# The first 256 columns of gate and up by token, one unit of sums for two, and another order of the splits, in a two-layer macaron block in fp32

## The chip, the cores and the metric

The kernel runs on one core of a Trainium2 chip. The metric is the device time of one execution in microseconds, as the median of several runs. Five engines share the work, each with a program of its own in fixed order: TensorE (PE) multiplies, VectorE (DVE) and ScalarE (ACT) do elementwise work and empty PSUM, GpSimd (POOL) does next to nothing here, and SyncE (SP) issues the loads. Semaphores alone tie them together, so an instruction that waits holds up everything behind it on its own engine.

## The reference

x has 256 tokens of 1024 features, everything is fp32, and there are two layers. Each has a feed-forward, a mixer and a second feed-forward, all with a residual. What the change touches is the feed-forward, of which there are four:

```python
def rms_norm(x, g):
    y = xf * lax.rsqrt(jnp.mean(xf * xf, axis=-1, keepdims=True) + RMS_EPS)
    return (y * g.astype(jnp.float32)).astype(x.dtype)

def swiglu(x, w_gate, w_up, w_down):          # 1024 -> 2816 -> 1024
    return (jax.nn.silu(x @ w_gate) * (x @ w_up)) @ w_down

for layer in range(DEPTH):                    # DEPTH = 2
    x = x + 0.5 * swiglu(rms_norm(x, ffn_norm[layer, 0]), ...)
    h = rms_norm(x, mix_norm[layer])
    x = x + (hybrid_ab_mixer(h, ...) if layer % 2 == 0 else short_conv_mixer(h, ...))
    x = x + 0.5 * swiglu(rms_norm(x, ffn_norm[layer, 1]), ...)
return rms_norm(x, final_norm)
```

The hybrid mixer of layer 0 multiplies `gelu(u)` into chunks mixed over the tokens, and has an attention beside it; both are concatenated and projected.

## The kernel before

**Products in parts.** A product in fp32 is made of products of rounded parts. Every weight tile of 1 MB is loaded raw by SP, rounded to `whi` by ACT (`Weights.high`, L91), and what the rounding left is taken to `wlo` by DVE (`Weights.low`, L96). The activations have the same two parts. With x as the stationary operand (`mm_n`, L290) a product takes three matmuls of 512 columns: hi by hi, hi by lo, lo by hi. With the weights stationary (`mm_t`, L267) it takes one of 512 columns (both parts of x at once) and one of 256.

**The stream of weights.** All weight tiles stand in one list of `Item`s. `W.next()` hands out the next one, and first issues the high parts of three items ahead and the low parts of two (`catch_up`, L106). There are five raw buffers; the low part of an item frees its buffer, and the next load goes into it. So the order of the list is the order of splits on ACT and DVE and of loads on SP. An item can also ask for sums of raw tiles, made on DVE (L87).

**A feed-forward.** Its 2816 columns of gate and up are 256 columns of an opening and five units of 512. The opening has the tokens along the free dimension (`open_pairs`, L439): two PSUM pairs, added (`added`, L417), scaled by the norm's root broadcast to all partitions (`Norm.broadcast`, L375: a product with the diagonal of the roots), gated and split (`gated`, L516). The units have the tokens on the partitions, so the root is a column there (`Norm.column`, L365) and scales within the evacuation (`silu` L540, `times` L537); then four transposes per pair of 128 columns turn the result (`turn`, L524), which is split for the down projection. A plain unit (`plain`, L543) has four items, and each of its four steps makes 24 matmuls. A unit of sums (`summed`, L565) is a Strassen-like form: seven steps of 12 matmuls, from four loads, seven splits, four sums of weights and sums of x (`Sums`, L473). `ORDER` (L37) interleaves the steps of three plain units ("n") and two of sums ("s"), and with them the items. Transposes are put into a list, `later`, from which one entry is run behind each step and, at the end, one ahead of each half of a down projection.

**The start.** The first feed-forward opens while x and the first weights land. SP issues pieces of 256 KB alternately; PE transposes x piece by piece (`turn_x`, L757), ACT and DVE split it and the weights (`prepare`, L764), and the opening's products run over eight slices of the features.

**PSUM.** Three tiles `ps` of two banks go round, and two tiles `misc` of one.

Of the kernel before, what the change touches and what calls it, by code (L numbers as in the profile page):

```python
# [36 lines left out]
ORDER = "nnsnsnsnssnsnsnsnsnssnsssn"  # L37
# [10 lines left out]
class Weights:  # L48
# [13 lines left out]
    def load_piece(self, i, s, e):  # L62
        name, src = self.src[i]
        if name not in self.raw:
            tag = self.free.pop(0)
            self.raw[name] = self.pool.tile(list(src.shape), F32, tag=tag, bufs=1, name="raw"), tag
            self.loaded = i + 1
        self.nc.sync.dma_start(self.raw[name][0][:, s:e], src[:, s:e])

    def load(self):  # L70
        while self.loaded < len(self.src) and self.free:
            self.load_piece(self.loaded, 0, self.src[self.loaded][1].shape[1])
# [59 lines left out]
def block_kernel(ctx: ExitStack, tc: tile.TileContext, a, out):  # L132
# [26 lines left out]
    def chunk(src):  # L159
# [8 lines left out]
    def sum_unit(g, u, c):  # L168
# [3 lines left out]
        yield Item([(b11, u[:, lo, c])], b11, drop=[])  # L172
        yield Item([(b12, g[:, lo, c])], b11, [(b11, b11, b12, ALU.subtract)], drop=[])
        yield Item([(b22, g[:, hi, c])], b11, [(b11, b11, b22, ALU.subtract)], drop=[])
        yield Item([], b22, drop=[])
        yield Item([], b12, [(b12, b12, b22, ALU.add)], drop=[b12, b22])
        yield Item([(b21, u[:, hi, c])], b21, drop=[])
# [5 lines left out]
    def ffn_items(l, s, natural):  # L183
        g, u, d = (cols(a[n][l, s]) for n in ("ffn_w_gate", "ffn_w_up", "ffn_w_down"))
        yield chunk(g[:, :, :256])
        yield chunk(u[:, :, :256])
        plain = (i for j in (0, 2, 4) for i in plain_unit(g, u, unit_cols(j)))
        sums = (i for j in (1, 3) for i in sum_unit(g, u, unit_cols(j)))
        for c in ORDER:
            yield next(plain if c == "n" else sums)  # L190
# [191 lines left out]

    def residual(norm, y, scale):
# [64 lines left out]
    def t_pair(xs, mid=None, mm=None, p=None):  # L448
        w, p = W.next(), p or ps()
# [57 lines left out]
    def ffn(norm, nxt, hooks=None, opened=None, squares=None):  # L507
        h = [None] * FB
        later = []
# [6 lines left out]
        def gated(g, u):  # L516
            s, v = (by_token(x, norm.rbc, tag) for x, tag in ((g, "ev_g"), (u, "ev_u")))
            nc.scalar.activation(s, s, AF.Silu)
            nc.vector.tensor_tensor(v, s, v, op=ALU.mult)
            h[:2] = split(v, 0, True)  # L520

        def turned(v, f, n):

            def turn(q):  # L524
                m = misc(1)
                for b in range(2):
                    for t in range(NT):
                        o = (2 * q + b) * P
                        nc.tensor.transpose(m[:, b * S + t * P:b * S + (t + 1) * P], v[t][:, o:o + P], ident)
                h[f + 2 * q:f + 2 * q + 2] = split(m, f + 2 * q)  # L530

# [89 lines left out]
        def first():  # L621
            gated(g0, u0)
# [543 lines left out]
```

## Time and profile before

| | |
|---|---|
| median of the runs (lowest, highest) | 951.05 us (950.37, 951.75) |
| the profiled execution, and its span | 951.3 us, 949.6 us |
| PE busy | 923.6 us, 97% |
| DVE busy | 728.3 us, 77% |
| ACT busy | 505.1 us, 53% |
| share of the chain that ended last: PE, DVE, ACT | 65%, 23%, 6% |

PE matmuls overlap in their ends, so a PE that counts as busy may still be held to less than its peak: what counts is the distance from one start to the next. The share of DVE is a mean over stages: it is near full in the feed-forwards' units and half idle in the down projections. The four feed-forwards begin at 0, 293.6, 478.8 and 755.4 us.

### The profile page before, as it was taken

The page shows a single profiled execution, that of the slowest core. Times are in us where ns is not written, and L with a number is a line of the kernel's source. Part 1 is how long each engine was busy: PE and PEld are TensorE (multiplying, and loading weights), DVE is VectorE, ACT ScalarE, POOL GpSimd, SP SyncE. Part 2 cuts the span into 40 slices and gives each one's busy share as a digit, 9 for nine tenths or more (in the row PEclk, how much of TensorE's full clock was granted, in tenths as well). Part 3 has the DMA queues.
Part 4 walks back from the last instruction along what each step waited for, and adds up shares of the span by engine and source line. Part 5 has one row for each costly group of instructions (what it writes and reads, how often), then busy time and mean ns, then how long its engine had stood idle before and what let it go on. Part 6 is the DMA issues. An engine that isn't in the chain of part 4 may idle for free.

```text
span 949.6 us, 11856 instructions
## 1 busy us (share of the span) xinstructions
PE 923.6 (97%) x4916; PEld 788.6 (83%) x4916; DVE 728.3 (77%) x740; ACT 505.1 (53%) x510; POOL 2.0 (0%) x9
## 2 busy tenths in 40 slices
PE   8889999999999999999999999999999999999997
PEld 7668788888988777888888788888999888788786
DVE  6998996466768989885669899664587789999562
ACT  6656564354847646553455665443444465656342
POOL 0000000000000000000000000000000000000000
PEclk9999999999999999999999999999999999999999
DMA  9439286646354446585544465847445533838511
GB/s 326 162 99 324 89 287 195 226 156 233 104 175 133 132 172 227 170 284 167 200 151 137 155 241 167 278 159 242 155 162 185 196 111 124 297 124 283 182 67 45
DMA packets 121169, 173.82 MB, mean 183 GB/s; under 512 B 3408, under 2 KB 69532, under 8 KB 121116
## 3 DMA queue, kind: packets, MB, share of 16 engines
q1 hardware_dynamic: 120780, 172.53, 54.2%
q8 instruction: 38, 0.62, 0.3%
q10 hardware_dynamic: 336, 0.54, 0.2%
q14 instruction: 15, 0.12, 0.0%
HBM read 172.01 MB, written 1.05 MB: 182 GB/s over the span
## 4 chain that ended last, share of the span: by engine, by line
PE 65%; DVE 23%; ACT 6%; issue 4%; DMA 1%; SPq 0%; DVEq 0%; ACTq 0%
PE ps L278 12%; DVE wlo L96 10%; PE ps L293 9%; PE ps L294 9%; PE ps L292 8%; PE ps L280 6%; DVE raw L87 4%; PE ps L286 3%; PE ps L287 3%; PE ps L288 3%; PE ps L270 2%; PE misc L294 2%; PE misc L292 2%; PE misc L293 2%; ACT whi L91 2%
## 5 line engine op out<-in xcount | busy, mean ns | idle before, releaser
L96 DVE TENSOR_TENSOR wlo<-raw,whi 128x2048 fp32r<-128x2048 f32 (+2 forms) x196 | 422.9, 2175 | 23.3 <-ACT whi L91 23.1
L91 ACT ACTIVATE whi<-raw 128x2048 fp32r<-128x2048 f32 (+2 forms) x196 | 354.2, 1824 | 160.4 <-PE ps L278 44.7
L293 PE MATMUL ps<-wlo,x 128*128 128x512 f32 x512 | 200.7, 392 | 4.7 <-DVE wlo L96 4.7
L292 PE MATMUL ps<-whi,x 128*128 128x512 f32 x512 | 203.0, 396 | 0.0
L294 PE MATMUL ps<-whi,x 128*128 128x512 f32 x512 | 200.2, 391 | 0.0
L278 PE MATMUL ps<-hx,whi 128*128 128x512 f32 x528 | 166.8, 397 | 0.0
L280 PEld LDWEIGHTS ps<-hx,wlo 128*128 128x128 f32 x528 | 99.2, 188 | 23.4
L293 PEld LDWEIGHTS ps<-wlo,x 128*128 128x128 f32 x512 | 96.6, 189 | 26.3 <-DVE wlo L96 7.0
L294 PEld LDWEIGHTS ps<-whi,x 128*128 128x128 f32 x512 | 96.4, 188 | 20.4
L292 PEld LDWEIGHTS ps<-whi,x 128*128 128x128 f32 x512 | 96.6, 189 | 19.7
L280 PE MATMUL ps<-hx,wlo 128*128 128x256 f32 x528 | 103.8, 278 | 0.0
L386 DVE SCALAR_TENSOR_TENSOR xT<-ps,xT 128x512 f32<-128x512 f32 x40 | 27.4, 690 | 69.3 <-PE ps L280 61.3
L278 PEld LDWEIGHTS ps<-hx,whi 128*128 128x128 f32 x528 | 80.4, 189 | 0.0
L87 DVE TENSOR_TENSOR raw<-raw 128x2048 f32<-128x2048 f32 x32 | 73.2, 2288 | 2.7 <-DMA raw<-in_ffn_w_gate 2.2
L286 PE MATMUL ps<-x,whi 128*128 128x256 f32 x224 | 64.0, 286 | 0.0
L287 PE MATMUL ps<-x,whi 128*128 128x256 f32 x224 | 63.4, 283 | 0.0
L288 PE MATMUL ps<-x,wlo 128*128 128x256 f32 x224 | 63.4, 283 | 0.0
L404 DVE TENSOR_TENSOR hx<-misc,hx 128x512 fp32r<-128x512 f32 x40 | 27.5, 689 | 32.5 <-ACT hx L401 32.5
L270 PE MATMUL ps<-x,whi 128*128 128x512 f32 x128 | 45.4, 398 | 0.8 <-ACT whi L91 0.6
L287 PEld LDWEIGHTS ps<-x,whi 128*128 128x128 f32 x224 | 43.0, 192 | 0.0
L286 PEld LDWEIGHTS ps<-x,whi 128*128 128x128 f32 x224 | 42.9, 192 | 0.0
L288 PEld LDWEIGHTS ps<-x,wlo 128*128 128x128 f32 x224 | 42.9, 192 | 0.0
(244 smaller groups left out, 1130.1 us busy)
## 6 DMA issues: line engine op xcount, KB each, us to landing
raw<-in_ffn_w_gate SPq DMA_DIRECT2D x43, 1024.0 KB, 5.3
raw<-in_ffn_w_up SPq DMA_DIRECT2D x43, 1024.0 KB, 5.2
raw<-in_ffn_w_down SPq DMA_DIRECT2D x34, 1024.0 KB, 6.4
raw<-in_conv_w_in SPq DMA_DIRECT2D x12, 1024.0 KB, 5.3
raw<-in_hyb_w_in SPq DMA_DIRECT2D x10, 1024.0 KB, 6.7
raw<-in_ffn_w_down SPq DMA_DIRECT2D x12, 768.0 KB, 4.9
raw<-in_hyb_w_out SPq DMA_DIRECT2D x4, 1024.0 KB, 5.4
raw<-in_conv_w_out SPq DMA_DIRECT2D x4, 1024.0 KB, 5.8
```

The costliest lines, as they stand in the source:

```text
L87: self.nc.vector.tensor_tensor(self.raw[dst][0], self.raw[x][0], self.raw[y][0], op=op)
L91: self.nc.scalar.activation(self.part(i, "whi")[:, s:e], self.tile(i)[:, s:e], AF.Copy)
L96: self.nc.vector.tensor_tensor(lo[:, s:e], raw[:, s:e], hi[:, s:e].bitcast(F32), op=ALU.subtract)
L270: nc.tensor.matmul(dst, whi, x, start=start, stop=False, skip_group_check=True)
L278: nc.tensor.matmul(dst, ws[i][0], xs[i], start=start and i == 0, stop=False, skip_group_check=True)
L280: nc.tensor.matmul(dst[:, :S], ws[i][1], xs[i][:, :S], start=False, stop=stop and i == n - 1, skip_group_check=True)
L286: nc.tensor.matmul(dst[:, :S], whi, x[:, :S], start=start, stop=False, skip_group_check=True)
L287: nc.tensor.matmul(dst[:, :S], whi, x[:, S:], start=False, stop=False, skip_group_check=True)
L288: nc.tensor.matmul(dst[:, :S], wlo, x[:, :S], start=False, stop=stop, skip_group_check=True)
L292: nc.tensor.matmul(dst, xhi, whi, start=start, stop=False, skip_group_check=True)
L293: nc.tensor.matmul(dst, xhi, wlo, start=False, stop=False, skip_group_check=True)
L294: nc.tensor.matmul(dst, xlo, whi, start=False, stop=stop, skip_group_check=True)
```

## The change

Four things change.

1. The opening is made like the units, with the tokens on the partitions. An item of the opening is four slices of gate and up side by side (2 x 256 columns, two loads), and `opening` makes 3 matmuls of 512 columns per slice and token block. The result is scaled by the column of roots as it leaves PSUM (`first`: two `silu`, two `times` of 256 columns), and turned by four transposes. The broadcast goes from the four feed-forwards; in the later ones the column root now stands right behind the opening. The sums of x are made later in the first feed-forward.
2. The first feed-forward has four plain units and one of sums. Its order is `"nnnsnnsnnsnnsnnsnnsnnsn"`; the other three keep the old one.
3. At the down projection the left transposes come behind the first half, two sets at once, and alternate between the two `misc` tiles.
4. In the hybrid mixer the first gated half is made inside `mix`. The hooks of the first feed-forward (small loads, angles, tables) move to earlier steps.

```diff
-ORDER = "nnsnsnsnssnsnsnsnsnssnsssn"
+ORDERS = {"first": ((0, 1, 2, 4), (3,), "nnnsnnsnnsnnsnnsnnsnnsn"),
+          "other": ((0, 2, 4), (1, 3), "nnsnsnsnssnsnsnsnsnssnsssn")}
...
     def ffn_items(l, s, natural):
-        yield chunk(g[:, :, :256])
-        yield chunk(u[:, :, :256])
...
+        for k in range(0, KB, 4):
+            yield chunk(g[:, k:k + 4, :256], u[:, k:k + 4, :256])
...
+    def opening(norm, p, k, w):
+        for t in range(NT):
+            mm_n(p[:, t], x_at(norm, t, k), (w[0][:, k % 4], w[1][:, k % 4]), k == 0, k == KB - 1)
...
-            later.extend([None] * n + [lambda: turn(0)] + [None] * (2 - n) + [lambda: turn(1)])
+            fns = [lambda q=q: turn(v, f + 2 * q, q, misc(1 - q * free[0])) for q in range(2)]
+            later.extend([None] * n + fns[:1] + [None] * (2 - n) + fns[1:])
...
-        pairs = opened or open_pairs(norm.x)
-        if not opened:
+        if opened is not None:
+            p0 = opened
+        else:
+            p0 = ps()
+            for k in range(KB):
+                if k % 4 == 0:
+                    w = W.next(later=k > 0)
+                opening(norm, p0, k, w)
+            W.flush(W.used + 2)
             xs.gained()
             xs.make(0)
+            norm.column()
             xs.make(1)
-        g0, u0 = (added(p, tag) for p, tag in zip(pairs, ("ev_g", "ev_u")))
...
         def first():
-            gated(g0, u0)
+            for t in range(NT):
+                silu(s[:, t], p0[:, t, :S], t)
+            for t in range(NT):
+                times(p0[:, t, S:], t, v[:, t], s[:, t])
+            later.extend([None] * (opened is None) + [lambda: turn([v[:, t] for t in range(NT)], 0, 0, misc(1))])
...
-            head = {0: [squares, xs.gained], 1: [norm.column, lambda: xs.make(0)], 2: [norm.broadcast, first],
-                    3: [lambda: xs.make(1)]}
+            head = {0: [squares], 1: [norm.column, first], 2: [xs.gained], 3: [lambda: xs.make(0)], 4: [lambda: xs.make(1)]}
         else:
-            head = {0: [norm.column], 1: [norm.broadcast], 2: [first]}
+            W.catch_up()
+            head = {0: [first]}
...
-        later[:] = [fn for fn in later if fn is not None]
+        rest = [fn for fn in later if fn is not None]
+        later[:] = [None, lambda: [fn() for fn in rest[:-2]]] + rest[-2:]
+        free[0] = 1
...
     for c in range(2):
         turn_x(c, misc())
         prepare(c)
-    opened = [(tuple(W.part(i, tag) for tag in ("whi", "wlo")), ps()) for i in range(2)]
+    opened = ps()
+    p = ps()
+    for c in range(2, KB // 2):
+        turn_x(c, p[:, c - 2])
     for k in range(KB):
-        t_step(opened, k, norm.x[k], k == 0, k == KB - 1)
+        if k in (0, 4):
+            w = [W.part(k // 4, tag) for tag in ("whi", "wlo")]
+        opening(norm, opened, k, w)
         if k == 1:
-            p = ps()
-            for c in range(2, KB // 2):
-                turn_x(c, p[:, c - 2])
             for c in range(2, KB // 2):
                 prepare(c)
...
             mixed.append(m)
+            if c == 0:
+                cat.extend(gated(0, u0))
...
-    cat = gated(0, u0) + gated(1, gate(u_ps)) + heads
+    cat += gated(1, gate(u_ps)) + heads
```

On SP the first loads stood as x, gate, x, up, gate, x, x, up, gate, up, gate, up; they stand now as x, gate, up, x, gate, up, x, x, gate, up, gate, up.

What the change moves on the engines is shown at three places. The rows name line, instruction, output and inputs; the number behind `whi` or `wlo` is the item's place in the list of weights.

PE at the start, before: four transposes of x, four more, then the products of the opening (the other eight transposes stand 16 matmuls later).

```order
L760 MATMUL misc_119<-ident_69,xin_90 128x128 x4
L760 MATMUL misc_138<-ident_69,xin_90 128x128 x4
L270 MATMUL ps_153<-x0_128,whi0_124 128x512
L271 MATMUL ps_153<-x0_128,wlo0_126 128x256
L270 MATMUL ps_153<-x0_128,whi0_124 128x512
```

PE at the start, now:

```order
L780 MATMUL misc_119<-ident_69,xin_90 128x128 x4
L780 MATMUL misc_134<-ident_69,xin_90 128x128 x4
L780 MATMUL ps_154<-ident_69,xin_90 128x128 x8
L299 MATMUL ps_153<-whi0_124,x0_128 128x512
L300 MATMUL ps_153<-wlo0_126,x0_128 128x512
L301 MATMUL ps_153<-whi0_124,x0_128 128x512
```

All sixteen transposes of x now stand ahead of the first product of the opening.

DVE in the first feed-forward, from the diagonals of the roots on, before (`xs` and `xp` are sums of x and their parts, `raw<-raw,raw` a sum of weights, `ev_g` and `ev_u` the opening's gate and up, `hx0` the split of the gated pair):

```order
L373 TENSOR_SCALAR diag_384<-ident_69,rstd_369 128x128 x2
L492 TENSOR_TENSOR xs0_333<-xg1_324,xg0_323 128x512
L502 TENSOR_TENSOR xp0_388<-xs0_333,xp0_388 128x512
L96 TENSOR_TENSOR wlo6_396<-raw_194,whi6_335 128x2048
L87 TENSOR_TENSOR raw_194<-raw_194,raw_279 128x2048
L426 TENSOR_TENSOR ev_g_267<-ev_g_267,rbc_414 128x512
L426 TENSOR_TENSOR ev_u_270<-ev_u_270,rbc_414 128x512
L519 TENSOR_TENSOR ev_u_270<-ev_g_267,ev_u_270 128x512
L96 TENSOR_TENSOR wlo7_424<-raw_262,whi7_394 128x2048
L404 TENSOR_TENSOR hx0_420<-ev_u_270,hx0_420 128x2x256
```

The same place now:

```order
L380 TENSOR_SCALAR diag_340<-ident_69,rstd_325 128x128 x2
L545 SCALAR_TENSOR_TENSOR v_344<-ps_153,rstd_325,s_343 128x256 x2
L102 TENSOR_TENSOR wlo6_351<-raw_187,whi6_293 128x2048
L93 TENSOR_TENSOR raw_145<-raw_145,raw_250 128x2048
L419 TENSOR_TENSOR hx0_389<-misc_384,hx0_389 128x2x256
L102 TENSOR_TENSOR wlo7_409<-raw_237,whi7_349 128x2048
L507 TENSOR_TENSOR xs0_402<-xg1_393,xg0_392 128x512
L517 TENSOR_TENSOR xp0_427<-xs0_402,xp0_427 128x512
L102 TENSOR_TENSOR wlo8_432<-raw_145,whi8_407 128x2048
L545 SCALAR_TENSOR_TENSOR v_458<-ps_297,rstd_325,s_380 128x512
```

The opening leaves PSUM by two multiplications right behind the root, and the first sum of x stands behind them and behind item 7.

DVE in the second feed-forward, from the diagonals on, before (items 59 to 61 are the fourth to sixth behind the opening):

```order
L373 TENSOR_SCALAR diag_2550<-ident_69,rstd_2535 128x128 x2
L96 TENSOR_TENSOR wlo59_2555<-raw_2295,whi59_2502 128x2048
L96 TENSOR_TENSOR wlo60_2592<-raw_2273,whi60_2553 128x2048
L87 TENSOR_TENSOR raw_2273<-raw_2273,raw_2500 128x2048
L426 TENSOR_TENSOR ev_g_2490<-ev_g_2490,rbc_2586 128x512
L426 TENSOR_TENSOR ev_u_2493<-ev_u_2493,rbc_2586 128x512
L519 TENSOR_TENSOR ev_u_2493<-ev_g_2490,ev_u_2493 128x512
```

The same place now, where item 55 is the first of sums:

```order
L380 TENSOR_SCALAR diag_2459<-ident_69,rstd_2444 128x128 x2
L509 SCALAR_TENSOR_TENSOR xs0_2435<-xs0_2435,xg0_2425 128x512
L517 TENSOR_TENSOR xp1_2463<-xs0_2435,xp1_2463 128x512
L102 TENSOR_TENSOR wlo55_2470<-raw_2241,whi55_2466 128x2048
L93 TENSOR_TENSOR raw_2241<-raw_2241,raw_2314 128x2048
L545 SCALAR_TENSOR_TENSOR v_2499<-ps_2366,rstd_2444,s_2498 128x256 x2
L102 TENSOR_TENSOR wlo56_2506<-raw_2263,whi56_2468 128x2048
```

The root has moved ahead of the second sum of x and of two splits, and the multiplications that empty the opening's PSUM stand behind one split and one sum of weights.

## Rows read from the trace of the kernel before

**Rows 1.** The page's first part: busy time of each engine, share, instructions.

```profile
PE 923.6 (97%) x4916; PEld 788.6 (83%) x4916; DVE 728.3 (77%) x740; ACT 505.1 (53%) x510; POOL 2.0 (0%) x9
```

**Rows 2.** Waits of PE, whole span: total us, times, longest.

```profile
PE ps L293 <- DVE wlo L96: 4.7, 5, 1.6
PE misc L529 <- DVE hx L404: 3.6, 5, 1.1
PE misc L378 <- DVE diag L373: 3.0, 3, 1.4
...
PE ps L270 <- DVE hxc L404: 0.6, 1, 0.6
```

**Rows 3.** Busy us by stage: window, length, PE, PEld, DVE, ACT, POOL, clock, DMA.

```profile
20.40:72.80 52.40, 45.83 (x197) 36.31 (x196) 46.29 (x50) 33.07 (x38) 0.00 (x0) 0.97 0.45 155
72.80:140.20 67.40, 65.64 (x298) 53.62 (x297) 63.53 (x61) 39.03 (x33) 0.64 (x1) 1.00 0.68 225
```

**Rows 4.** Waits of PE from 20 to 160 us.

```profile
PE misc L529 <- DVE v L538: 2.6, 2, 2.3
PE ps L293 <- DVE wlo L96: 2.4, 2, 1.6
PE misc L529 <- DVE hx L404: 1.5, 2, 0.9
```

**Rows 5.** Timeline of PE, units of the first feed-forward: start, us, line, tiles.

```profile
43.48 0.39 PE L292 MATMUL ps<-whi,xp 128*128 128x512 f32 x1
...
46.20 0.39 PE L292 MATMUL ps<-whi,x 128*128 128x512 f32 x1
48.17 0.50 PE L293 MATMUL ps<-wlo,x 128*128 128x512 f32 x1 [1.59 <-DVE wlo L96]
...
59.76 0.77 PE L292 MATMUL ps<-whi,x 128*128 128x512 f32 x1
...
63.18 0.39 PE L294 MATMUL ps<-whi,x 128*128 128x512 f32 x1
...
69.57 0.60 PE L529 MATMUL misc<-ident,v 128*128 128x128 f32 x4
```

**Rows 6.** Timeline of PE, second feed-forward.

```profile
293.61 0.40 PE L270 MATMUL ps<-x,whi 128*128 128x512 f32 x1
...
317.04 0.70 PE L378 MATMUL misc<-diag,ones 128*128 128x256 f32 x2 [0.78 <-DVE diag L373]
317.38 0.58 PE L292 MATMUL ps<-whi,x 128*128 128x512 f32 x1
```

**Rows 7.** Timeline of PE, the start.

```profile
11.03 1.04 PE L760 MATMUL ps<-ident,xin 128*128 128x128 f32 x8
...
20.39 0.40 PE L292 MATMUL ps<-whi,x 128*128 128x512 f32 x1
```

**Rows 8.** Timeline of ACT, the start.

```profile
7.66 1.38 ACT L91 ACTIVATE whi<-raw 128x512 fp32r<-128x512 f32 x2 [1.48 <-DMA raw<-in_ffn_w_up]
...
10.66 1.38 ACT L91 ACTIVATE whi<-raw 128x512 fp32r<-128x512 f32 x2 [0.90 <-DMA raw<-in_ffn_w_up]
```

**Rows 9.** The page's groups: busy us, mean ns of one, idle before and releaser.

```profile
L96 DVE TENSOR_TENSOR wlo<-raw,whi 128x2048 fp32r<-128x2048 f32 (+2 forms) x196 | 422.9, 2175 | 23.3 <-ACT whi L91 23.1
L91 ACT ACTIVATE whi<-raw 128x2048 fp32r<-128x2048 f32 (+2 forms) x196 | 354.2, 1824 | 160.4 <-PE ps L278 44.7
...
L87 DVE TENSOR_TENSOR raw<-raw 128x2048 f32<-128x2048 f32 x32 | 73.2, 2288 | 2.7 <-DMA raw<-in_ffn_w_gate 2.2
...
L404 DVE TENSOR_TENSOR hx<-misc,hx 128x512 fp32r<-128x512 f32 x40 | 27.5, 689 | 32.5 <-ACT hx L401 32.5
```

**Rows 10.** Timeline of DVE, second feed-forward: the root's first operation.

```profile
314.54 0.15 DVE L305 TENSOR_SCALAR rs_v<-misc 128x2 f32<-128x2 f32 x1
```

**Rows 11.** Loads: KB each, us from issue to landing; whole span, then 0 to 15 us.

```profile
raw<-in_ffn_w_gate SPq DMA_DIRECT2D x43, 1024.0 KB, 5.3
...
raw<-in_ffn_w_up SPq DMA_DIRECT2D x2, 1024.0 KB, 10.9
```

More of the change, by code (lines that the diff above doesn't have):

```diff
@@ L65, in load_piece @@
             tag = self.free.pop(0)
-            self.raw[name] = self.pool.tile(list(src.shape), F32, tag=tag, bufs=1, name="raw"), tag
+            shape = [P, src[0].shape[1], sum(part.shape[2] for part in src)]
+            self.raw[name] = self.pool.tile(shape, F32, tag=tag, bufs=1, name="raw"), tag
             self.loaded = i + 1
-        self.nc.sync.dma_start(self.raw[name][0][:, s:e], src[:, s:e])
+        at = 0
+        for part in src:
+            self.nc.sync.dma_start(self.raw[name][0][:, s:e, at:at + part.shape[2]], part[:, s:e])
+            at += part.shape[2]
     def load(self):
         while self.loaded < len(self.src) and self.free:
-            self.load_piece(self.loaded, 0, self.src[self.loaded][1].shape[1])
+            self.load_piece(self.loaded, 0, self.src[self.loaded][1][0].shape[1])
     def tile(self, i):
@@ L184, in ffn_items @@
         g, u, d = (cols(a[n][l, s]) for n in ("ffn_w_gate", "ffn_w_up", "ffn_w_down"))
-        yield chunk(g[:, :, :256])
-        yield chunk(u[:, :, :256])
[L187 to L190, printed above, removed]
+        for k in range(0, KB, 4):
+            yield chunk(g[:, k:k + 4, :256], u[:, k:k + 4, :256])
+        plain, summed, order = ORDERS["other" if l or s else "first"]
+        steps = {"n": (i for j in plain for i in plain_unit(g, u, unit_cols(j))),
+                 "s": (i for j in summed for i in sum_unit(g, u, unit_cols(j)))}
+        for c in order:
+            yield next(steps[c])
         if natural:
@@ L381, in broadcast, with x_at @@
             self.rbc2 = self.rbc.to_broadcast([P, 2, S])
+    def x_at(norm, t, d):
+        return tuple(half(norm.x[d], j)[:, t * P:(t + 1) * P] for j in range(2))
+    def opening(norm, p, k, w):
+        for t in range(NT):
+            mm_n(p[:, t], x_at(norm, t, k), (w[0][:, k % 4], w[1][:, k % 4]), k == 0, k == KB - 1)
     def residual(norm, y, scale):
@@ L508, in ffn @@
         h = [None] * FB
-        later = []
+        later, free = [], [0]
         def run_later():
@@ L514, in run_later, with turn @@
                 fn()
[L516 to L520, printed above, removed]
-        def turned(v, f, n):
[L524 to L530, printed above, removed]
-            later.extend([None] * n + [lambda: turn(0)] + [None] * (2 - n) + [lambda: turn(1)])
-        def x_at(t, d):
-            return tuple(half(norm.x[d], j)[:, t * P:(t + 1) * P] for j in range(2))
+        def turn(v, f, q, m):
+            for b in range(2):
+                for t in range(NT):
+                    o = (2 * q + b) * P
+                    nc.tensor.transpose(m[:, b * S + t * P:b * S + (t + 1) * P], v[t][:, o:o + P], ident)
+            h[f:f + 2] = split(m, f)
+        def turned(v, f, n):
+            fns = [lambda q=q: turn(v, f + 2 * q, q, misc(1 - q * free[0])) for q in range(2)]
+            later.extend([None] * n + fns[:1] + [None] * (2 - n) + fns[1:])
         def times(u, t, dst, src):
```

56 lines of the change are left out of this document (28 added, 28 removed).

## The prediction

> **What bounds the kernel now.** I read the page's engine totals first: TensorE (PE) is busy 97% of the span [rows 1], so the time is PE's work plus the holes in it. PE's waits come next: the four kinds that the change is near have 11.9 us, all released by VectorE (DVE) [rows 2]. Third, where they lie: in the units of the first feed-forward PE is idle 6.6 us of the first stretch and 1.8 of the second, 8.3 us in all, while DVE is busy 46.29 of 52.40 and 63.53 of 67.40 us [rows 3], and its waits there are for v, for low parts and for hx [rows 4]. So in the first feed-forward DVE sets the pace and PE follows; in the three later ones PE does, with a few waits of 0.5 to 1.1 us. An edit that frees DVE is worth much in the first; in the others it is worth the waits, and PE's own instructions count in full.
>
> PE's prices: twelve products of 512 columns from 43.48 to 46.20, so 0.2267 us each. A hole costs more than it lasts: the wait of 1.59 us that ends at 48.17 puts 1.97 between two starts, 0.16 above hole and product. Four transposes are busy 0.60 us, and the next product starts under their end; with its slower start I take 0.46 [rows 5].
>
> **First feed-forward, PE's work.** A plain unit is 96 products, a unit of sums 84, so one unit changed over adds 12: +2.7 us. The broadcast goes, with its two passes and the restart behind them: -0.45 (0.34 from 317.04 to 317.38 [rows 6], and a late second product). Four transposes of the gated pair come: +0.46. The Trainium skill, "TensorE: Matmul & The Clock Gate", section Back-to-back issue gap, gives about 131 ns for a product of 512 columns in a sustained stream. By that the 12 products would cost an estimated 1.6 us and the total would be 1.1 us less; the row says 0.2267 and decides.
>
> **First feed-forward, the start.** Before, the products run from the eight transposes at 11.03 on without a break, with a quarter of the opening done earlier, to its end at 20.39 [rows 7]. Now all transposes of x stand ahead of the first product, and x's last piece is the eighth load on SP's queue. Before, the fourth load ended a wait of ScalarE (ACT) at 7.66, the eighth one at 10.66 [rows 8]. Loads of the same size in the same rhythm should land alike: x's last piece at about 10.66, its transposes, the first product at 11.1. 48 x 0.2267 = 10.9 gives 22.0 for the end of the opening, against 20.39: +1.6 us. The splits don't hold it: they follow the loads by 1 to 3 us, and the last two slices of x are needed only at 19.3.
>
> With it goes PE's clock. PE will stand nearly idle from 5.3 to 11.1. Before, behind the hole of 2.3 us [rows 4], eight products took 3.42 us (59.76 to 63.18 [rows 5]) instead of 1.81, most of them at the 1.2 GHz level, and the granted clock of that stretch is 0.97 [rows 3]; the hole of 1.59 had no such effect. I put 1.4 us on the opening (bounds: 0, if the transposes keep the clock up, and 9.6, if all 48 products run at the slow pitch of 3.42 / 8 = 0.43). The start costs 3.0 us in all.
>
> **First feed-forward, what DVE gets back.** A unit of sums has seven splits (L96, 2.2 us each on DVE) and four sums of weights (L87, 2.29) [rows 9]; a plain unit has four splits. One unit changed over saves 3 x 2.2 + 4 x 2.2 = 15.4 us of DVE and its additions. The opening saves two additions, two products with the broadcast root and the gating (5 x 0.69, like L404's operations of that size [rows 9]) for two multiplications of half the width (not in the trace; between 0.35 and 0.69, and I take 0.45): -2.5. DVE loses 18 us of work where PE waited 8.3.
>
> Does it lose them early enough? The tight place is the low part of item 10. On DVE, counted from the start of the root: root and first diagonal 2.2, the two multiplications done by 3.4; low parts 6 to 10, 11.0; two sums of weights 4.4; hx twice 1.2; three sums of x with their low parts 3.6; three waits for ACT's high parts, 0.7 each and 1.0 more where ACT is in item 8; two products v 1.3. Together 28.0. PE from the same moment: items 4 to 9, 120 products, 27.2, and three sets of transposes, 1.4: 28.6. DVE is there 0.6 us earlier, and from there on a step costs it less than PE. So I let the waits go and put 0.3 us for this place (bounds 0 and 3, the latter if ACT's high parts come a split later).
>
> What goes: the holes, 8.3 [rows 3]; 0.16 for each of some eight, 1.3; the slow clock, 1.6. Sum up to the down projection: -11.2 + 2.7 - 0.45 + 0.46 + 3.0 + 0.3 = **-5.2**.
>
> **The three later openings.** Before, the second feed-forward takes 23.77 us from the opening's first product (293.61) to the first product of sums (317.38) [rows 6]. Now: 48 products 10.88, the column root 0.36, two plain steps 10.88, so the first sums could start at 315.73. They reuse the opening's PSUM, so they wait for its two multiplications on DVE. There the root starts 0.3 behind the column, at 305.2, and takes 2.4 with the diagonals (314.54 [rows 10] to the end of PE's wait for them, 317.0): 307.6. The sum of x 0.6, ACT's high part 0.7, the low part 0.65: 309.6. ACT splits item 5 only behind that high part (1.8 [rows 9]): 310.8; low part 313.0, sum of weights 315.2, the two multiplications 316.1. A new wait of 0.3, and 1.3 gained. ACT's table load for Silu, ahead of the multiplications in the second feed-forward alone, ends under the sum of weights. The fourth is like the second (-1.3); the third had no wait for the diagonals and gains 0.5. Sum -3.1; the three sets of transposes +1.4.
>
> At the later splits DVE's lead over PE grows by about 1.9 us (2.6 less work, 0.7 less time on PE). That covers the waits for a low part there: of the 4.7 us in five [rows 2], two with 2.4 are in the first feed-forward [rows 4]; the other three hold 2.3, and with two short ones and the restarts 3.1: -3.1. Without that cover these 3.1 stay.
>
> **Down projections and hybrid.** At the four entries to a down projection the turned pairs now alternate between two PSUM tiles and come behind the first products. PE's waits for hx, 3.6 us in five, of which one of 0.9 lies earlier [rows 2, 4], leave 2.7, with restarts 3.3, less 0.4 left over: -2.9. In the hybrid mixer the first gated half is made one step earlier, behind the first mixed pair: PE's 0.6 us for hxc [rows 2] and its restart, -0.8. The small loads move ahead on SP; they queue while item 12 still waits for its buffer: nothing.
>
> Sum: -5.2 - 3.1 + 1.4 - 3.1 - 2.9 - 0.8 = -13.7. The profiled execution took 951.3 us (span 949.6), 0.25 above the median of the runs; the changed kernel should profile at 937.6 and have a median of **937.3 us**.
>
> **The rivals.**
> - DVE still sets the pace in the first third. For it: a margin of 0.6 us in 28, on a list with three waits for ACT. Against it: PE's waits are DVE's lead afterwards. 3 us there and half of the 3.1 later: 937.3 + 2.7 + 1.6 = 941.6.
> - The clock stays at its low level through the opening. For it: behind 2.3 us of idling PE ran 3.4 us at the slow pitch, and here it idles longer. Against it: it rose again behind eight dense products. 937.3 + (9.6 - 1.4) = 945.5. The Trainium skill, "TensorE: Matmul & The Clock Gate", Part 1, says the throttled clock is the default and sustained activity releases it; by that rule the loss ends with the first dense products, and the trace agrees (eight of them).
> - The opening's PSUM comes free late in the later feed-forwards: its multiplications stand behind a split and a sum of weights. If ACT's high part comes one split later, three waits of 2.2: 943.9.
> - Slower: the weights starve. The unit of sums holds three of the five raw buffers from item 11 to 17, so the six plain items 12, 13, 15, 16, 18, 19 stream through two. A round of a buffer is load, high part, low part: 5.3 [rows 11] + 1.8 + 2.2 = 9.3 us, and two buffers give an item in 4.7 us, while PE takes one in 6.8. Holes begin beyond a round of 13.6; beyond 19 the kernel is slower than before. With the 10.9 us that loads took in the first rush [rows 11] and 3 us of queueing before each split a round is 20.9: 6 x (10.45 - 6.8) = 21.9, so 959.2. Against it: that rush had three times as many loads under way.
> - That DVE's list isn't shortened at all is excluded by the order: 15.4 us of its instructions are gone by name.
>
> **How the numbers follow.** The forecast with its small variants (933.5 to 940) has 0.62, DVE in the first third 0.16, the clock 0.08, late PSUM 0.07, starving 0.04, and 0.03 that several gains fall short together, to no change. To leave out no more than 2 in 10 the range goes from 933.5 (no clock loss, no new waits, x landing 1 us earlier) to 943.0. Faster by over 0.2%, about what a measurement of this kernel can tell from no change: 0.93; same 0.03; slower 0.04.
>
> **What would show it.** Right: the opening's first product near 11.1, the first plain product at 22 to 24, the down projection at about 135; at most one wait for a low part over 0.5 us behind 30; in the later feed-forwards 22.2 to 22.7 us from the opening's first product to the first sums; no wait for hx at the entries. Wrong: a slow pitch past 16 us, PE waiting for DVE between 45 and 72, PE waiting for the opening's multiplications, or DVE waiting for loads between 60 and 90.

## The result

The changed kernel takes 938.39 us (median of four runs, 937.99 to 938.47) where the kernel before took 951.32 in the same session (median of four; the 951.05 from which the forecast starts is the median of the first three): a ratio of 0.9865 with a 95% interval of 0.9848 to 0.9882. The forecast was 937.3, the range 933.5 to 943.0. The profiled execution took 938.33 us with a span of 936.6.

The page's totals, and the groups of VectorE's (DVE's) splits and sums of weights, to be held against [rows 1, 9]:

```profile
PE 925.6 (99%) x4872; PEld 790.7 (84%) x4872; DVE 700.8 (75%) x712; ACT 493.9 (53%) x494; POOL 2.0 (0%) x9
...
L102 DVE TENSOR_TENSOR wlo<-raw,whi 128x2048 fp32r<-128x2048 f32 (+2 forms) x189 | 415.6, 2217 | 27.2 <-ACT whi L97 27.1
...
L93 DVE TENSOR_TENSOR raw<-raw 128x2048 f32<-128x2048 f32 x28 | 64.1, 2288 | 3.2 <-DMA raw<-in_ffn_w_gate 2.9
```

TensorE (PE) is busy 99% of the span instead of 97, and DVE has seven splits and four sums of weights less. All of PE's waits in the whole span (total, times, longest), where [rows 2] had 11.9 us released by DVE:

```profile
PE ps L780 <- DMA xin<-in_x: 1.5, 1, 1.5
PE misc L780 <- DMA xin<-in_x: 1.2, 1, 1.2
PE misc L771 <- DVE ones L240: 1.1, 1, 1.1
```

Those three lie in the first 10 us; the view lists none for DVE behind them. The two stretches of the first feed-forward (the columns of [rows 3]) have no hole and no low clock left:

```profile
20.40:72.80 52.40, 52.40 (x239) 43.11 (x238) 42.73 (x46) 32.18 (x37) 0.64 (x1) 1.00 0.55 190
72.80:134.28 61.48, 61.48 (x282) 50.68 (x281) 46.38 (x50) 31.85 (x27) 0.00 (x0) 1.00 0.68 230
```

PE's timeline gives the marks that the prediction named: the opening's first products, the first plain product (23.20), the first down projection (134.28), and the second feed-forward from its opening (286.49) to its first product of sums (309.04), which stands 0.49 us behind the product before it.

```profile
10.86 0.77 PE L299 MATMUL ps<-whi,x 128*128 128x512 f32 x1
11.43 0.63 PE L300 MATMUL ps<-wlo,x 128*128 128x512 f32 x1
11.86 0.63 PE L301 MATMUL ps<-whi,x 128*128 128x512 f32 x1
...
13.90 0.40 PE L300 MATMUL ps<-wlo,x 128*128 128x512 f32 x1
...
23.20 0.39 PE L299 MATMUL ps<-whi,x 128*128 128x512 f32 x1
...
134.28 0.40 PE L285 MATMUL ps<-hx,whi 128*128 128x512 f32 x1
...
286.49 0.39 PE L299 MATMUL ps<-whi,x 128*128 128x512 f32 x1
...
308.55 0.39 PE L301 MATMUL ps<-whi,x 128*128 128x512 f32 x1
309.04 0.47 PE L299 MATMUL ps<-whi,x 128*128 128x512 f32 x1
```

The two multiplications that let go of the opening's PSUM there, on DVE:

```profile
308.02 0.87 DVE L545 SCALAR_TENSOR_TENSOR v<-ps,rstd,s 128x256 f32<-128x256 f32 x2
```

The first feed-forward reaches its down projection 5.9 us earlier (140.20 [rows 3] to 134.28), the second takes 22.55 us from opening to sums instead of 23.77 [rows 6].

So far all goes by the book. But the sum does not close: from the first down projection on the other stages give 7.1 us more, and that hides a cost of nearly 4 us which no step of the prediction has. The experiments find it.

### The profile page after: what moved, and what is told of

The parts are those of the page before. It is cut to its first block, busy times and chain, and to the rows that moved or that the text cites. A ratio compares the mean times of both kernels' runs of the same rounds, so it can differ in the third digit from the quotient of the medians.

```text
span 936.6 us, 11741 instructions
## 1 busy us (share of the span) xinstructions
PE 925.6 (99%) x4872; PEld 790.7 (84%) x4872; DVE 700.8 (75%) x712; ACT 493.9 (53%) x494; POOL 2.0 (0%) x9
## 4 chain that ended last, share of the span: by engine, by line
PE 98%; DMA 1%; SPq 0%; DVE 0%; issue 0%; ACT 0%; DVEq 0%
PE ps L299 18%; PE ps L300 18%; PE ps L301 18%; PE ps L285 15%; PE ps L287 7%; PE ps L293 3%; PE ps L294 3%; PE ps L295 3%; PE misc L299 3%; PE misc L300 3%; PE misc L301 3%; PE misc L536 2%; PE ps L277 2%; PE ps L278 1%; DMA xin<-in_x 1%; PE misc L375 0%
## 5 line engine op out<-in xcount | busy, mean ns | idle before, releaser
L102 DVE TENSOR_TENSOR wlo<-raw,whi 128x2048 fp32r<-128x2048 f32 (+2 forms) x189 | 415.6, 2217 | 27.2 <-ACT whi L97 27.1
L97 ACT ACTIVATE whi<-raw 128x2048 fp32r<-128x2048 f32 (+2 forms) x189 | 348.5, 1857 | 162.4 <-PE ps L285 45.1
L299 PE MATMUL ps<-whi,x 128*128 128x512 f32 x600 | 237.2, 395 | 0.3
L300 PE MATMUL ps<-wlo,x 128*128 128x512 f32 x600 | 234.8, 391 | 0.0
L301 PE MATMUL ps<-whi,x 128*128 128x512 f32 x600 | 234.6, 391 | 0.0
L299 PEld LDWEIGHTS ps<-whi,x 128*128 128x128 f32 x600 | 113.1, 189 | 24.4 <-issue 1.5
L301 PEld LDWEIGHTS ps<-whi,x 128*128 128x128 f32 x600 | 112.9, 188 | 24.1
L300 PEld LDWEIGHTS ps<-wlo,x 128*128 128x128 f32 x600 | 113.1, 189 | 23.8 <-DVE wlo L102 1.1
L93 DVE TENSOR_TENSOR raw<-raw 128x2048 f32<-128x2048 f32 x28 | 64.1, 2288 | 3.2 <-DMA raw<-in_ffn_w_gate 2.9
L419 DVE TENSOR_TENSOR hx<-misc,hx 128x512 fp32r<-128x512 f32 x44 | 30.0, 689 | 28.9 <-ACT hx L416 28.9
L416 ACT ACTIVATE hx<-misc 128x512 fp32r<-128x512 f32 x44 | 25.5, 589 | 36.1 <-PE misc L536 36.1
```

The costliest lines, as they stand in the source:

```text
L93: self.nc.vector.tensor_tensor(self.raw[dst][0], self.raw[x][0], self.raw[y][0], op=op)
L97: self.nc.scalar.activation(self.part(i, "whi")[:, s:e], self.tile(i)[:, s:e], AF.Copy)
L102: self.nc.vector.tensor_tensor(lo[:, s:e], raw[:, s:e], hi[:, s:e].bitcast(F32), op=ALU.subtract)
L299: nc.tensor.matmul(dst, xhi, whi, start=start, stop=False, skip_group_check=True)
L300: nc.tensor.matmul(dst, xhi, wlo, start=False, stop=False, skip_group_check=True)
L301: nc.tensor.matmul(dst, xlo, whi, start=False, stop=stop, skip_group_check=True)
```

## The experiments

### The start: late transposes, and a busy TensorE

The kernel before, run again beside each group of these kernels, took 951.40 to 951.67 us; a few tenths between two kernels of different groups say nothing.

The prediction puts 3.0 us on the start, in two parts. One kernel moves the last transposes back behind two slices of the opening:

```diff
-    p = ps()
-    for c in range(2, KB // 2):
-        turn_x(c, p[:, c - 2])
     for k in range(KB):
 ...
         if k == 1:
+            p = ps()
+            for c in range(2, KB // 2):
+                turn_x(c, p[:, c - 2])
             for c in range(2, KB // 2):
                 prepare(c)
```

> The changed kernel with the last eight transposes of x behind the opening's first two slices, as before, instead of ahead of its first product. Theory A, the start costs what the prediction put on it (1.6 us because the first product waits for x's last piece, and most of 1.4 us for the clock): the first product of the opening at about 7 to 8.5 us instead of 10.86, the first plain product at about 20 instead of 23.2, and the 3 us stay, since VectorE's list behind the root starts earlier with TensorE: 935.4 us. Rival B, VectorE has no slack at item 10 (its low part ends at 63.50 us, and TensorE is there at 63.18): TensorE then waits there for most of the 3 us, 937.5 to 938.4. Rival C, the splits of the first slices come later than TensorE could start: gain of 1 us or less at the first plain product.

It took 936.62 us, 1.8 less than the changed kernel. PE's timeline: first product, the transposes, first plain product, first down projection.

```profile
7.56 0.78 PE L299 MATMUL ps<-whi,x 128*128 128x512 f32 x1
...
11.91 1.03 PE L780 MATMUL ps<-ident,xin 128*128 128x128 f32 x8
...
20.99 0.39 PE L299 MATMUL ps<-whi,x 128*128 128x512 f32 x1
...
132.04 0.40 PE L285 MATMUL ps<-hx,whi 128*128 128x512 f32 x1
```

The 2.2 us gained at the first plain product are still there at the down projection, and PE has no new wait. Theory A holds in kind, at 1.8 to 2.2 of its 3.0 us: PE takes 4.35 us for the first slices' twelve products, more than the 2.7 of the full pace. Rival B falls, though its place is real. These are the root's first operation and the low part of item 10 on DVE, and PE's two products there, in the changed kernel:

```profile
34.62 0.16 DVE L312 TENSOR_SCALAR rs_v<-misc 128x2 f32<-128x2 f32 x1 [2.80 <-PE misc L375]
...
61.21 2.29 DVE L102 TENSOR_TENSOR wlo<-raw,whi 128x2048 fp32r<-128x2048 f32 x1
```

```profile
63.18 0.48 PE L299 MATMUL ps<-whi,x 128*128 128x512 f32 x1
63.55 0.50 PE L300 MATMUL ps<-wlo,x 128*128 128x512 f32 x1
```

The low part ends at 63.50, and the product that reads it starts at 63.55. There is no slack, yet an earlier PE does not wait here, because the root that starts DVE's list waits for PE's column (the 2.80 us in its row): the whole list moves with PE. With late transposes the root starts at 32.41, the low part ends at 61.27 and the product starts at 61.33, all three 2.2 us earlier.

The other kernel keeps PE at work while it waits for x:

```diff
+    fill = ps(0)
 ...
+    def keep_busy(n):
+        for _ in range(n):
+            nc.tensor.matmul(fill[:, 0, :P], ones, ones, start=True, stop=True)
     for c in range(2):
         turn_x(c, misc())
+        keep_busy((6, 8)[c])
         prepare(c)
```

> The changed kernel with 6 products of ones behind the first eight transposes' first half and 8 behind its second half, into an unused bank, so that TensorE is not idle while it waits for x. Theory A, the opening's slow first products (48 in 12.34 us instead of 10.88) come from TensorE's idling before them: the granted clock is at its full level at the first product, the opening ends 1.4 us earlier, 937.0 us. Rival, the first products are slow for another reason or the clock stays low whatever runs before: opening 12.3 us, 938.4 us, or more if the added products delay a transpose.

It took 936.65 us, 1.7 less, by theory A. The opening's first products now stand 0.23 us apart, and the 48 take 10.98 us instead of 12.34:

```profile
10.38 0.48 PE L299 MATMUL ps<-whi,x 128*128 128x512 f32 x1
10.70 0.40 PE L300 MATMUL ps<-wlo,x 128*128 128x512 f32 x1
10.93 0.39 PE L301 MATMUL ps<-whi,x 128*128 128x512 f32 x1
...
21.36 0.39 PE L299 MATMUL ps<-whi,x 128*128 128x512 f32 x1
```

The changed kernel's products stand 0.43 us apart until 13.56, which is the pace of the 1.2 GHz level [rows 5]. Its trace's record of the clock begins only at 13.8 us, at the full level, so that a window before that reads 1.00 against the pace. Where the record covers such a start, in the kernel with 32 more bytes below, the same pace stands at a granted clock of 0.50; in the kernel that keeps PE at work it covers the whole opening and reads 1.00. The Trainium skill, "TensorE: Matmul & The Clock Gate", Part 1, says that activity releases the throttled clock; this pair of kernels agrees (0.43 us from product to product without the added ones, 0.23 with them).

### One unit of sums, with the old opening and with the new

The kernel before, with its second unit of sums changed for a plain one, and the small loads moved with it:

```diff
-ORDER = "nnsnsnsnssnsnsnsnsnssnsssn"
+ORDERS = {"first": ((0, 1, 2, 4), (3,), "nnsnnsnnsnnsnnsnnsnnsnn"),
+          "other": ((0, 2, 4), (1, 3), "nnsnsnsnssnsnsnsnsnssnsssn")}
 ...
```

> The kernel before with one unit of sums instead of two in its first feed-forward (a unit of sums' step behind every two plain ones, the small loads where the changed kernel has them); its opening, its other feed-forwards and the addresses of its hidden values stay. Theory A, VectorE's 15.4 us in that unit are what TensorE waits for, whatever the opening: of the 11.2 us of waits, restarts and slow clock some 15.4 / 18 go and 2.7 us of products come, 951.7 - 6.9 = 944.8 us. Rival, the old opening with its broadcast root keeps VectorE late by itself: 949 us or more.

It took 949.44 us against 951.45: 2.0 us, and theory A falls. All of PE's waits between 20 and 145 us:

```profile
PE misc L380 <- DVE diag L375: 3.0, 1, 3.0
PE misc L531 <- DVE hx L406: 1.7, 1, 1.7
```

The waits for low parts and for v [rows 4] are gone, as 15.4 us less on DVE should make them. But PE, coming earlier, now stands 3.0 us at the broadcast of the root (1.4 before [rows 2]), and 1.7 at the entry to the down projection. Around that first wait the granted clock is half (columns as in [rows 3]):

```profile
36.80:43.70 6.90, 6.22 (x15) 4.88 (x16) 5.98 (x10) 3.82 (x5) 0.00 (x0) 0.51 0.17 40
```

The twelve products behind the broadcast take 5.48 us (38.14 to 43.62) where the full pace would be 2.72. So the root, the entry and the clock take some 6 us back (1.6, 1.7 and 2.8) of what the shorter list of DVE sets free.

The converse is the changed kernel with two units in their old order:

```diff
-ORDERS = {"first": ((0, 1, 2, 4), (3,), "nnnsnnsnnsnnsnnsnnsnnsn"),
+ORDERS = {"first": ((0, 2, 4), (1, 3), "nnsnsnsnssnsnsnsnsnssnsssn"),
 ...
```

> The changed kernel with two units of sums in the first feed-forward again, in the old order of steps (and the small loads at the steps where they stood); the opening by token and all else stay. Theory A, VectorE's 15.4 us of splits and sums of weights in that unit are what made TensorE wait there: TensorE has 2.7 us less work and gets some 8 to 9 us of waits and restarts back in the first feed-forward, 943.5 to 945. Rival, the opening alone had taken the waits away: 2.7 us less than the changed kernel, 935.7 us.

It took 949.66 us, 11.3 more than the changed kernel and some 5 more than theory A had. PE's three largest waits for DVE and ScalarE (ACT), and its product behind the first of them:

```profile
PE ps L299 <- DVE v L545: 4.7, 1, 4.7
PE ps L299 <- ACT xp L516: 1.9, 1, 1.9
PE ps L300 <- DVE wlo L102: 1.7, 2, 1.0
```

```profile
38.97 0.77 PE L299 MATMUL ps<-whi,x 128*128 128x512 f32 x1 [4.74 <-DVE v L545]
```

That is the rival on late PSUM, in the first feed-forward instead of the later ones: the first step of sums, which is the third step in this order, wants the opening's tile before the root behind the second step has let go of it. And PE pays again, at half the clock from 37 us on (window, length, PE, PEld, DVE, ACT, POOL, clock, DMA):

```profile
37.00:43.70 6.70, 4.73 (x11) 3.80 (x12) 5.89 (x7) 2.64 (x3) 0.00 (x0) 0.50 0.38 143
```

So a third kernel puts the first step of sums at the fourth place (its order is "nnnsnsnsnssnsnsnsnsnssnsss"). In this order the transposes of the first unit of sums read their tile after the second unit has begun to overwrite it, so those values are other ones; the instructions are the same.

> The changed kernel with two units of sums in the first feed-forward, but with the first sum at its fourth step, where the changed kernel has it, and not at its third: there the sum waited 4.7 us for the opening's PSUM, behind the root. Theory A, VectorE's 15.4 us in the second unit of sums still cost more than the 2.7 us of products that it saves: 949.7 less 4.7 and some 1.2 of restart and slow clock, 943.8 us, with TensorE's waits for low parts at items 10 to 20 left. Rival, that one PSUM wait was the whole cost and the second unit is free in this order: 935.7 us.

It took 943.49 us, near theory A's 943.8; the down projection starts at 139.39, 5.1 us behind the changed kernel's. Of PE's waits the first belongs to the overwritten tile, 2.1 us with its restart on top; the second is the price of DVE's list:

```profile
PE misc L536 <- DVE r L586: 2.1, 1, 2.1
PE ps L300 <- DVE wlo L102: 1.9, 2, 1.2
```

The second unit of sums thus costs some 2.8 us where the order suits it (5.1 less 2.3, an estimate), its 2.7 us of saved products included; in the kernel before it costs 2.0. The first product behind the first down projection compares all five kernels at the same point of the work (the three with the new opening have the new entry too):

| kernel | units of sums | first product behind the first down projection | ahead of before |
|---|---|---|---|
| before | 2 | 204.06 | |
| before, one unit | 1 | 202.31 | 1.75 |
| new opening, old order | 2 | 208.60 | -4.54 |
| new opening, first sum a step later | 2 | 203.00 | 1.06 |
| after | 1 | 197.93 | 6.13 |

Without the wait at the overwritten tile the fourth row would be some 3.4 us ahead. With it the two edits alone make 1.75 and 1.06 of the 6.13; without it 1.75 and 3.4, which is 5.2. So how much the two edits need each other hangs on that tile: by this estimate they nearly add up. What is shown is that the order decides: the same opening with the same two units takes 949.66 or 943.49 us.

### The later openings, the entries, the hybrid mixer

Three kernels undo one part each. The old opening in the three later feed-forwards:

```diff
         else:
-            p0 = ps()
-            for k in range(KB):
-                if k % 4 == 0:
-                    w = W.next(later=k > 0)
-                opening(norm, p0, k, w)
 ...
+            pairs = open_pairs(norm.x)
 ...
-            head = {0: [first]}
+            head = {0: [norm.column], 1: [norm.broadcast], 2: [old_first]}
```

> The changed kernel with the opening of before (gate and up one after the other, turned, with the broadcast root) in the three later feed-forwards; the first one and all entries stay. Theory A, the prediction's terms: 3.1 us for the later openings and 3.1 us for their low parts come back, 1.4 us of transposes go, 943.2 us. Rival B, those terms were too small: by the stages of the changed kernel's trace, with the slower pitch of its hidden values' products taken out, the three later feed-forwards gained 9.5 us, of which the entries can hold 2.2: 945.7 us. Rival C, the openings were covered anyway: 938.4 us less the transposes, 937 us.

It took 945.64 us, 7.25 more. PE's waits for DVE in it:

```profile
PE ps L304 <- DVE wlo L102: 2.1, 3, 0.7
...
PE ps L303 <- DVE v L549: 1.6, 1, 1.6
PE misc L389 <- DVE diag L384: 1.4, 2, 0.7
```

The waits for low parts and diagonals of [rows 2] are back. The 1.6 us for v stand at 871.29, at the last down projection, and neither original has a wait for v there; they are put down to the mixture, which no run shows. Without them and their restart some 5.5 us are the later openings' and their cover's, between theory A's 4.8 and rival B.

The old handling of the pairs left over at the entries:

```diff
-        rest = [fn for fn in later if fn is not None]
-        later[:] = [None, lambda: [fn() for fn in rest[:-2]]] + rest[-2:]
-        free[0] = 1
+        later[:] = [fn for fn in later if fn is not None]
```

> The changed kernel with the turned pairs left over at the end of a feed-forward handled as before: from the first step of the down projection on, one at a time, through one PSUM tile. Theory A, the prediction's term: the waits for hx at the four entries come back, 0.7 us each with their restarts, 941.3 us. Rival, they stay away, since VectorE and ScalarE now come to the entry earlier: 938.4 us.

942.13 us, 3.7 more: theory A, a little larger. PE waits at each of the four entries:

```profile
PE misc L536 <- DVE hx L419: 2.6, 4, 1.1
```

And both gated halves of the hybrid mixer at its end (the two lines with cat.extend taken out):

> The changed kernel with both gated halves of the hybrid mixer made at its end, as before. Theory A, the prediction's term: TensorE waits 0.6 us for hxc and restarts, 0.8 us more, 939.2 us. Rival, ScalarE and VectorE come to that place earlier now and the wait stays away: 938.4 us.

939.41 us, 1.0 more; the wait is the one of [rows 2], to the tenth:

```profile
PE ps L277 <- DVE hxc L419: 0.6, 1, 0.6
```

### Where a tile lies: five microseconds for 32 bytes

The three undone parts and the first feed-forward make 5.9 + 5.5 + 3.7 + 1.0 = 16.1 us; the profiled executions lie 13.0 apart. The rest lies in the pace of products that wait for nothing. In the first down projection 304 products follow each other; from their first start to the next stage's first they took 53.03 us before and 53.54 after. No order and no shape there had changed. What had is the tiles' place: the changed kernel makes its tiles in another sequence, and the hidden values' (hx, and the sums of x, xp) stand 160 bytes further on, on multiples of 64. One kernel adds a tile of 32 bytes per partition ahead of them:

```diff
             v = act.tile([P, NT, S], F32, tag="ev_u", bufs=2, name="v")
+            if "pad" not in room:
+                room["pad"] = act.tile([P, 8], F32, tag="pad", bufs=1, name="pad")
+                nc.gpsimd.memset(room["pad"], 0.0)
```

> The changed kernel with one more tile of 32 bytes per partition in SBUF, so that the tiles of the hidden values (hx), which stand 160 bytes further on in the changed kernel than before, stand 32 bytes further still: at 32 bytes past a multiple of 64, as before, instead of on one. Nothing else moves in the order. Theory A, the address sets the pitch of the down projections' products: the 304 products behind the last transposes of the first down projection take 52.9 us from first to last start, as before, instead of 53.4; three such groups and two output projections give 1.7 us back, 936.7 us. Rival, the slower pitch has another cause (the order in which the pairs are made, work beside it): 53.4 us in that group and 938.4 us.

By the built program's table of addresses, hx, the sums of x and what they are made from move by 32 bytes, and behind them tiles of the mixers and the final norm; the weights and x stay. It took 933.23 us, 5.2 less than the changed kernel, three times what theory A had claimed from the old pace. PE's timeline around the 304 products (first, and first of the next stage) and around 72 products of the last down projection, in the changed kernel:

```profile
144.39 0.48 PE L285 MATMUL ps<-hx,whi 128*128 128x512 f32 x1
...
197.93 0.39 PE L299 MATMUL ps<-whi,x 128*128 128x512 f32 x1
...
884.39 0.48 PE L299 MATMUL ps<-whi,hx 128*128 128x512 f32 x1
...
901.28 0.28 PE L299 MATMUL misc<-whi,hx 128*128 128x256 f32 x1
```

and in the kernel with 32 bytes more:

```profile
144.68 0.48 PE L285 MATMUL ps<-hx,whi 128*128 128x512 f32 x1
...
197.46 0.39 PE L299 MATMUL ps<-whi,x 128*128 128x512 f32 x1
...
881.28 0.48 PE L299 MATMUL ps<-whi,hx 128*128 128x512 f32 x1
...
897.85 0.28 PE L299 MATMUL misc<-whi,hx 128*128 128x256 f32 x1
```

53.54 us become 52.78, and 16.89 become 16.57. Over the whole traces the three groups of 304 give 2.3 us, the products of 512 columns with hx or xp stationary 2.0, and the last down projection's 128 products of 256 columns 0.8 (15.35 to 14.51). Two more kernels look for the rule: 64 bytes in that place instead of 32, and 32 bytes in the kernel before, which put its tiles on multiples of 64.

> The changed kernel with 64 bytes more per partition ahead of the hidden values, not 32: they stand 64 bytes past a multiple of 128. Theory A, it is the multiple of 64 that is slow: as the changed kernel, 53.4 us for the 304 products and 938.4 us. Rival, every placing modulo 128 has a pitch of its own (before stands at 96, the changed kernel at 0, the one with 32 bytes at 32): a time apart from the 938.4 and 933.2 us of those by a microsecond or more.

> The kernel before with 32 bytes more per partition ahead of its evictions' and hidden values' tiles, so that hx stands on a multiple of 64 bytes (of 128 too), as in the changed kernel. Theory A, the address sets the pitch: the 304 products of the first down projection take 53.4 us from first to last start instead of 52.9, and the kernel 4.0 us more (in the changed kernel 501 products of 512 columns with hx or the sums of x held at 233.2 ns instead of 228.1, 2.6; the down projections' three quarters at 1.3, 3.7 and 1.5 ns more, 1.8; less 0.4 in the output projections): 955.5 us. Rival, the pitch belongs to something else in the changed kernel: 52.9 us there and 951.5 us.

They took 938.43 and 951.53 us (before: 951.40). The same two stretches in all five placings (the place from the built program's table of addresses):

| kernel | hx, bytes past a multiple of 128 | 304 products, hx moving | last 72 products, hx stationary |
|---|---|---|---|
| before | 96 | 53.03 | 16.45 |
| before, 32 bytes more | 0 | 52.79 | 16.88 |
| after | 0 | 53.54 | 16.89 |
| after, 32 bytes more | 32 | 52.78 | 16.57 |
| after, 64 bytes more | 64 | 53.48 | 16.88 |

With 64 bytes more all is as with none, so the rival of that run falls. Where the tile is the stationary operand of 512 columns, a multiple of 64 costs 4 to 6 ns a product in all five placings. Where it is the moving one, the changed kernel's three placings follow the same rule, but the kernel before does not: on a multiple of 64 it is fast. So theory A of the last run falls for the down projections (52.67 us from first to last start, not 53.4), and with it its sum of 955.5. That the place of the tiles sets the pace is shown, for the stationary operand with a rule. What else decides for the moving one stays open: modulo 128 the padded kernel before and the changed kernel stand alike and still differ by 0.75 us in that group. By the same table the one's hx starts on a multiple of 4096 bytes and the other's 128 bytes past one; no run tests whether that matters.

Why the slower products of the padded kernel before hardly show in its time can be read from the two traces, stage by stage. The feed-forwards' units and the last down projection, where the tiles are stationary, take 2.0 us longer; the three groups of 304 and the two output projections, where they move, take 1.2 less (0.24 and 0.25 each). The profiled executions lie 0.65 apart, the medians 0.1.

### Three edits at once

> The changed kernel with three edits at once: the tile of 32 bytes ahead of the hidden values, the last eight transposes of x behind the opening's first two slices, and 8 products of ones behind the first four transposes. Theory A, address, late x and clock are three separate costs: the opening's first slices run at 0.2267 us a product from 7.5 us on, its first plain product stands at 19.5 us instead of 23.2, and the gain of the address (5.2 us) comes on top: 929.7 us. Rival B, with the start that early VectorE's low parts hold TensorE at item 2 (it ends at 19.95 us) and at item 10: only as much as late x alone gives, 931.5 us. Rival C, the address gives its gain only by chance of one placing and nothing here: 935 us.

930.62 us, a ratio of 0.9779 (0.9765 to 0.9792) to before, and 7.8 us less than the changed kernel: theory A, less 0.9. It beats both kernels. All of PE's waits, and its first plain product:

```profile
PE misc L774 <- DVE ones L240: 1.1, 1, 1.1
PE ps L299 <- DVE v L545: 0.4, 2, 0.2
PE ps L300 <- DVE wlo L102: 0.4, 1, 0.4
```

```profile
20.66 0.39 PE L299 MATMUL ps<-whi,x 128*128 128x512 f32 x1
```

The first plain product comes at 20.66, not 19.5: the opening's first product stands at 7.88, not 7.5, and the second waits 0.4 us for its own low part and starts 0.9 us behind it.

## Why the prediction was right, point by point

- **Start, +3.0:** 2.8 (20.39 [rows 7] to 23.20). The first product at 10.86 for 11.1, and the clock's part 1.46 (12.34 for 10.88) where 1.4 was forecast. Each of the two causes was taken away by itself.
- **The tight place:** DVE's list took 28.9 us (34.62 to 63.50) for 28.0, PE 28.9 for 28.6. The lead of 0.6 us that the prediction had is gone: the low part ends 0.05 us ahead of its product. No wait worth the name came of it, and the 0.3 us put there were not paid, but only just.
- **First feed-forward, -5.2:** -5.9. But the step from DVE's 18 us to PE's 8.3 is right only of both edits together. The prediction did not ask what either does alone: one unit less in the kernel before gave 2.0 us, where the same step makes 6.9 (the expectation of that run), because PE then waits at the root and loses its clock there. The new opening has no broadcast to wait for.
- **Later openings, their low parts and transposes, -3.1 - 3.1 + 1.4:** about -5.5, and 1.22 us from opening to sums in the second where 1.3 was forecast. The new wait of 0.3 us is there: in each of the three the first product of sums stands 0.49 us behind its predecessor, 0.26 more than the pace. DVE's two multiplications end at 308.89, 22.4 us behind the opening's first product, where the prediction had 22.5. The rival of three waits of 2.2 did not come here, though with two units of sums in the first feed-forward such a wait took 4.7 us.
- **Entries, -2.9, and hybrid, -0.8:** -3.7 and -1.0. Waits cost a few tenths more than the hole and 0.16.
- **What failed** is the sentence that prices every product of 512 columns at 0.2267 us. It was read from twelve products with xp as the stationary operand [rows 5], while xp lay 32 bytes past a multiple of 64, and the change moved xp and hx. On x, whose tiles did not move, the mean stayed (227.5 and 227.7 ns). Those with hx or xp as the stationary operand took 228.1 ns before and 233.2 after (mean distance of two starts, 501 of them after: 2.6 us), the three long down projections 0.50 us each more, the output projections 0.2 less in all: 3.9 us. The total came out within 1.1 us because the waits were priced some 2.4 us too low (16.1 for 13.7); 0.8 us between the parts and the whole stay unassigned. Two errors of opposite sign, neither of which the range was made for.
- **Rivals:** none of the five came true. Behind 20 us the view lists no wait of PE for weights or low parts, and the slow pitch ends at 13.9.

## What to carry to other kernels

Where two engines take turns as the bound, don't turn work saved on one into time of the other at a fixed rate: 15.4 us less on VectorE paid 2.0 us alone (2.7 us of added products taken off), because PE that comes early at one place waits at the next, here at the root, and ran at half its clock there. Before crediting or blaming an order, compare the pace of long runs of products that wait for nothing; if it differs with the same instructions, shift the tiles by 32 bytes and measure. And a TensorE that waits for the first loads is worth keeping busy: 14 products of ones gave 1.7 us.

## What was not expected of the hardware

- 32 bytes in SBUF ahead of the hidden values change the kernel by 5.2 us (938.39 to 933.23) with the same instructions in the same order beside one memset: a stationary operand on a multiple of 64 bytes costs 234 to 235 ns a product of 512 columns where 32 bytes past it costs 228 to 230 (16.89, 16.88 and 16.88 us against 16.45 and 16.57 for 72 products). That is 2.0 of the 5.2 us; for the rest, products in which the tile moves or of 256 columns, no rule was found.
- Transposes with waits between them do not keep the clock up for the products behind them. In the kernel with 32 bytes more the granted clock reads half over the last transposes and the first products, and full from there on (columns as in [rows 3]):

```profile
7.60:14.30 6.70, 4.79 (x17) 4.03 (x16) 5.06 (x8) 4.61 (x9) 0.00 (x0) 0.50 1.07 366
14.40:20.00 5.60, 5.60 (x26) 4.62 (x25) 5.60 (x8) 5.03 (x7) 0.00 (x0) 1.00 1.05 387
```
